# Expert blocks summed in threes, gathers left out of the gates, and part of VectorE's top-k work given to GpSimd

## The chip, the cores and the metric

The kernel runs on one core of one Trainium2 chip, in one launch. The metric is the device time of one execution in microseconds (us). One execution was recorded by the hardware profiler; its rows are the trace. The engines are named as in the profile: PE is TensorE (PEld its weight loads), DVE is VectorE, ACT is ScalarE, POOL is GpSimd, SP is SyncE, which only issues transfers. A q behind the name (POOLq) is the engine's instruction queue. Every engine works through its own queue in order.

## The reference

A decoder layer over x of 1024 tokens by 1024 features. A conditioning vector gives shifts, scales and gates. A first half mixes the tokens (a gated linear recurrence and a short convolution) and adds the result to x. The second half, where the change lies, looks experts up by product keys:

```python
q = (xb @ w_query).reshape(T, PEER_HEADS, 2, PEER_HALF)          # 8 heads, 2 halves of 128
s = jnp.einsum('thpk,hpnk->thpn', q, sub_keys).astype(jnp.float32)  # 128 keys per half
top_s, top_i = lax.top_k(s, PEER_TOPK)                            # 16 of 128
cand_s = top_s[:, :, 0, :, None] + top_s[:, :, 1, None, :]
cand_i = top_i[:, :, 0, :, None] * PEER_NKEYS + top_i[:, :, 1, None, :]
best_s, best_pos = lax.top_k(cand_s.reshape(T, PEER_HEADS, PEER_TOPK * PEER_TOPK), PEER_TOPK)
idx = jnp.take_along_axis(cand_i.reshape(...), best_pos, axis=-1)
gate = jax.nn.softmax(best_s, axis=-1)
u = expert_u[idx]
v = expert_v[idx]
act = jax.nn.gelu(jnp.einsum('td,thkd->thk', xb, u).astype(jnp.float32), approximate=False)
return jnp.einsum('thk,thkd->td', (gate * act).astype(xb.dtype), v)
```

There are 16384 experts (128 by 128), each with a row of 1024 floats in u and one in v; a token uses 128 of them. A last norm follows.

## The kernel before

**Two ways for the tokens.** 640 tokens (TD) go the dense way: u and v of all experts are multiplied for all of these tokens, in 128 blocks of 128 experts, and a matrix of gates that is zero for experts not chosen weighs them. The other 384 tokens go by gathers, in 3 groups of 128: for each of a token's 128 experts an indirect DMA on GpSimd's queue brings the u row (L1095, into one of five row buffers, `grow` and `more`), VectorE multiplies it with the token's h and sums it into `aw` (L1113), and likewise a v row is gathered and added into `gacc` (L1105). That is 384 u steps and 384 v steps of 0.52 MB each. They are written by a generator, `background()`, which other code moves on by `advance(cost)`: with a rate for each stage (RE in the queries, RF in the gates, RG in the tail), and in the main stage by `along`, which spreads what is still left evenly over the matmul columns (`per_column`).

**Products.** A product of two fp32 tiles is three float32r matmuls (high by high, high by low, low by high). `halves_of` makes the halves: ACT copies the raw tile into the high part (L113), DVE subtracts it to get the low part (L114). Names with h and l at the end are such halves: `wh, wl` (or `wxh, wxl` from another pool) of a query weight or of a block of u, `vh, vl` of a block of v, `Wh, Wl` of a block of weighted activations.

**Stages** (names used below, with their place in the trace):
- queries (714 to 857 us): 16 query matrices for the dense tokens, 48 matmuls each on PE (L889), then scores, then the top 16 of 128 on DVE for five tiles of 128 tokens (`top16`, L936 to L940).
- top-k (857 to 989): for each tile the candidates (`candidates`), then softmax, then `digits` for all five tiles in one (it takes the two index digits out of the best positions, in ops of 640 elements), then `pick` for each tile: a one-hot (L1006), a product (L1008), a tree of additions (L1011, L1013). Meanwhile PE computes u blocks that are done early (`u_early`, L1165): 40 of the 128 blocks (EARLIES, every b with b % 3 == 1), stored as `ged` and reloaded in the main stage.
- gates (989 to 1338): ten quarters of 64 tokens. DVE makes one-hots and products (`lo`, `hi`, `O1` at L1303, `P` at L1309), PE multiplies them (L1318, 128 matmuls a quarter), ACT evicts to `stg` and stores to `gd`. Early u blocks and, by RF, gathers are mixed in.
- tail (1338 to 1366): what is left of the early blocks.
- main (1366 to 2989): the u products of the other 88 blocks (L1165), `w_step` (gelu by gate, halves `Wh, Wl`), `v_load` (halves `vh, vl`), and after every SB blocks a `v_phase` that adds Wh, Wl by vh, vl (L1383) for five tiles of tokens: three in PSUM (`pacc`), two through `pa` into `acc0` and `acc2` (L1393). `Wh, Wl, vh, vl` have SLOTS high-part buffers. A phase is written when the next block's W and v have been made.
- end (2989 to 3003).

Order within an engine's queue is set by a scheduler from dependencies and costs; `keep_in_program_order` ties the gathers' steps to the order in which the generator writes them.

Of the kernel before, what the change touches and what calls it, by code (L numbers as in the profile page):

```python
# [7 lines left out]
F32 = mybir.dt.float32  # L8
# [6 lines left out]
OP = mybir.AluOpType  # L15
# [4 lines left out]
P = 128  # L20
S = 1024
DM = 1024
KC = DM // P
# [7 lines left out]
NK = 128  # L31
# [4 lines left out]
DT = -(-TD // P)  # L36
# [2 lines left out]
NG = len(GG)  # L39
FULL = REST // P  # L40
assert REST % P == 0 and TD % P == 0
SB = 4
GB = 4
TG = 64 if TD % 64 == 0 else 32
NTG = TD // TG
GSCALE = 2.0 ** 15
EARLY = 40
EARLIES = [b for b in range(NK) if b % 3 == 1][:EARLY]
SLOTS = SB + 1
ROWS = 4  # L50
TB = 8
NE = 3.6
NF = 2.1
MID = 1
WL = 3
# [22 lines left out]
WH = 3  # L78
WA = 1
RE = 0.1  # L80
RF = 0.9
RG = 0.5
RATES = {"B": RB, "D": RD, "E": RE, "F": RF, "G": RG}
SPREAD = 0.97
# [13 lines left out]
def build(tc, A, out, dbg=None):  # L98
# [9 lines left out]
            return st.enter_context(tc.tile_pool(name=name, bufs=bufs, reuse_waits="tile", **kw))  # L108
        return st.enter_context(tc.tile_pool(name=name, bufs=bufs, side=side, reuse_waits="tile", **kw))

    def split(hi, lo, src):

        C.activation(hi, src, AF.Copy)  # L113
        V.tensor_tensor(lo, src, hi.bitcast(F32), op=OP.subtract)  # L114

    def raw_tile(pl, shape, name, lb):

        return pl.tile(shape, F32R, name=name + "l", bufs=lb).bitcast(F32)

    def halves_of(pl, raw, shape, name, lb, hb):  # L120
        hi = pl.tile(shape, F32R, name=name + "h", bufs=hb)
        lo = pl.tile(shape, F32R, name=name + "l", bufs=lb)
        split(hi, lo, raw)
        return hi, lo

    def rsqrt(r, v, tmp, e=0):
# [13 lines left out]
    with root:  # L140
# [37 lines left out]
        up = pool(stQ, "up", side="right")  # L178
# [17 lines left out]
        def fetch(n):  # L196
            if n < len(order) and n not in raws:
                src, i = order[n]
                raws[n] = raw_tile(up, [P, KC, P], "w", WL)
                SY.dma_start(raws[n], A[src][i])  # L200

        def halve(n):

            if n < len(order) and n not in halves:
                fetch(n)
                if n in extra:
                    halves[n] = halves_of(extra[n], raws[n], [P, KC, P], "wx", 1, 1)
                else:
                    halves[n] = halves_of(up, raws[n], [P, KC, P], "w", WL, 2)

        def deepen(pl, first, n, every):

# [782 lines left out]
            V.tensor_copy(code, ci)  # L995
            return pf, code

        def pick(new, ab, ti, dst):

            w = ti.shape[0]  # L1000
            tib = new("tib", [2, TOPK, HEADS], BF16)
            V.tensor_copy(tib, ti.rearrange("p (h c) a -> p c a h", c=2))
            sh = [w, TOPK, TOPK, HEADS]
            for c in range(2):
                oh = new("oh", [TOPK, TOPK, HEADS], BF16)
                V.tensor_tensor(oh, ab[c][:, :, None, :].to_broadcast(sh),  # L1006
                                iota16[:w, None, :, :].to_broadcast(sh), op=OP.is_equal)
                V.tensor_tensor(oh, oh, tib[:, c, None, :, :].to_broadcast(sh), op=OP.mult)  # L1008
                n = TOPK // 2
                while n > 1:  # L1010
                    V.tensor_tensor(oh[:, :, :n], oh[:, :, :n], oh[:, :, n:2 * n], op=OP.add)  # L1011
                    n //= 2
                V.tensor_tensor(dst[c], oh[:, :, 0], oh[:, :, 1], op=OP.add)  # L1013
                yield 3.5

        def norm_store(pl, o, w, parts, fw, r, sq, queue=None):
# [200 lines left out]
        scores.pop()()  # L1217

        def new(name, shape, dt):
            return qp.tile([P] + shape, dt, name=name, bufs=1)  # L1220

        fill = [0.0, 0.0]

        def early_along(steps_):
            for c in steps_:
                fill[0] += c * NE / 26.0
                if fill[0] - fill[1] > 0.25:
                    u_early(fill[0] - fill[1], "E")
                    fill[1] = fill[0]
# [2 lines left out]
        bp = new("bp", [DT, HEADS, TOPK], U32)  # L1232
        for t in range(DT):
            early_along(candidates(new, lambda v, m, a, b: top16(qp, v, m, a, b), ts[:, t], bs[:, t], bp[:, t]))
        softmax(new, bs, gk)
        ab = digits(new, bp)
        early_along([8.0])
        for t in range(DT):
            early_along(pick(new, [a[:, t] for a in ab], ti[:, t], [i1[:, t], i2[:, t]]))
        stE.close()  # L1240


# [259 lines left out]
```

## Time and profile before

| what | value |
|---|---|
| time, median of 3 runs | 3003.61 us (2998.58 to 3007.3) |
| the profiled execution: time, span in the trace | 3004.52 us, 3002.8 us |
| mean granted TensorE clock | 0.955 |
| busy over the span: PE, DVE, ACT, POOL | 2751.3 us (92%), 2451.9 us (82%), 933.6 us (31%), 1029.8 us (34%) |
| moved by DMA | 767.20 MB, mean 255 GB/s |

The span runs from the first to the last instruction; 1.7 us of the profiled execution lie outside it. A busy share is an average over the stages; the limits differ from stage to stage.

### The profile page before, as it was taken

How to read it: one execution, taken by the hardware profiler on the slowest of the kernel's cores; microseconds unless marked ns; L12 is line 12 of the kernel's file. 1: busy time of each engine (PE TensorE's matmuls, PEld its weight loads, DVE VectorE, ACT ScalarE, POOL GpSimd, SP SyncE). 2: the span in 40 equal slices, each digit the busy share in tenths (PEclk: the TensorE clock that was granted, in tenths of full speed). 3: DMA queues.
4: the chain of work that ended last, by engine and by line, in shares of the span. 5: the costliest groups of instructions: out<-in, count | busy, mean ns of one | idle time of the engine just before them, and what ended most of it. 6: DMA issues, size and time to landing. Idle time of an engine off the chain costs nothing.

```text
span 3002.8 us, 41579 instructions
## 1 busy us (share of the span) xinstructions
PE 2751.3 (92%) x15683; PEld 2432.8 (81%) x15683; DVE 2451.9 (82%) x4997; ACT 933.6 (31%) x1553; POOL 1029.8 (34%) x816
## 2 busy tenths in 40 slices
PE   8999999997999978777999999999999999999998
PEld 5887787877999877676888888888888888888887
DVE  6875529999999989986787878788878788887788
ACT  4643645433222433322222222222121222121222
POOL 0000000000000055553555455555545555555452
PEclk8999999989999988888999999999999999999999
DMA  7424342234234599999898898899888888988885
GB/s 267 148 85 138 132 138 77 71 102 165 64 100 135 198 365 380 374 356 355 314 328 317 296 325 316 316 332 332 321 323 300 311 322 329 334 312 309 311 307 216
DMA packets 249034, 767.20 MB, mean 255 GB/s; under 512 B 23553, under 2 KB 75777, under 8 KB 242434
## 3 DMA queue, kind: packets, MB, share of 16 engines
q0 software_dynamic: 115296, 419.48, 39.0%
q1 hardware_dynamic: 83202, 286.87, 27.2%
q10 hardware_dynamic: 50336, 58.20, 5.5%
q8 instruction: 122, 2.00, 0.3%
q14 instruction: 78, 0.64, 0.1%
HBM read 696.31 MB, written 68.16 MB: 255 GB/s over the span
## 4 chain that ended last, share of the span: by engine, by line
PE 41%; DVE 20%; DMA 15%; issue 15%; POOL 4%; ACT 3%; ACTq 1%; SPq 0%; DVEq 0%; POOLq 0%
PE pacc L1383 10%; PE pa L1383 8%; PE pp L466 7%; PE pa L1165 7%; DMA Wl<-ged 3%; DVE wl L114 3%; DMA wl<-in_uT 2%; DVE gacc L1105 2%; DMA vl<-in_v 2%; PE ps L588 1%; DVE vl L114 1%; PE pp L732 1%; DMA wl<-in_wq 1%; DVE s L938 1%; DVE P L1309 1%
## 5 line engine op out<-in xcount | busy, mean ns | idle before, releaser
L1165 PE MATMUL pa<-h2h,wh 128*128 128x320 f32 x1840 | 582.6, 317 | 44.4 <-ACT ge L1170 32.0
L1165 PE MATMUL pa<-h2h,wl 128*128 128x320 f32 x1840 | 578.3, 315 | 5.1 <-DVE wl L114 5.1
L1165 PE MATMUL pa<-h2l,wh 128*128 128x320 f32 x1840 | 580.3, 315 | 0.0
L1165 PEld LDWEIGHTS pa<-h2h,wh 128*128 128x128 f32 x1840 | 353.7, 192 | 52.4 <-ACT ge L1170 35.2
L1165 PEld LDWEIGHTS pa<-h2h,wl 128*128 128x128 f32 x1840 | 353.2, 192 | 6.3 <-DVE wl L114 6.3
L1165 PEld LDWEIGHTS pa<-h2l,wh 128*128 128x128 f32 x1840 | 354.1, 192 | 2.0
L1383 PE MATMUL pacc<-vh,Wh 128*128 128x512 f32 x768 | 304.7, 397 | 55.0 <-ACT Wh L113 46.4
L113 ACT ACTIVATE wh<-wl 128x1024 fp32r<-128x1024 f32 x187 | 198.0, 1059 | 442.8 <-DMA wl<-in_uT 183.5
L1383 PE MATMUL pacc<-vl,Wh 128*128 128x512 f32 x768 | 301.8, 393 | 0.1
L1383 PE MATMUL pacc<-vh,Wl 128*128 128x512 f32 x768 | 300.3, 391 | 0.1
L114 DVE TENSOR_TENSOR wl<-wl,wh 128x1024 fp32r<-128x1024 f32 x187 | 228.0, 1220 | 75.0 <-ACT wh L113 71.6
L113 ACT ACTIVATE vh<-vl 128x1024 fp32r<-128x1024 f32 x128 | 135.0, 1054 | 370.6 <-PE pacc L1383 297.1
L1383 PE MATMUL pa<-vh,Wh 128*128 128x512 f32 x512 | 206.0, 402 | 24.3 <-ACT Wh L113 22.3
L1383 PEld LDWEIGHTS pacc<-vh,Wh 128*128 128x128 f32 x768 | 145.8, 190 | 92.6 <-ACT Wh L113 55.0
L113 ACT ACTIVATE Wh<-Wl 128x640 fp32r<-128x640 f32 x128 | 94.5, 739 | 380.0 <-DVE Wl L1360 264.7
L1383 PE MATMUL pa<-vl,Wh 128*128 128x512 f32 x512 | 203.9, 398 | 0.0
L1383 PE MATMUL pa<-vh,Wl 128*128 128x512 f32 x512 | 203.3, 397 | 0.0
L1383 PEld LDWEIGHTS pacc<-vh,Wl 128*128 128x128 f32 x768 | 144.9, 189 | 30.8 <-DVE Wl L114 0.8
L1383 PEld LDWEIGHTS pacc<-vl,Wh 128*128 128x128 f32 x768 | 145.8, 190 | 29.5 <-DVE vl L114 0.8
L114 DVE TENSOR_TENSOR vl<-vl,vh 128x1024 fp32r<-128x1024 f32 x128 | 155.0, 1220 | 4.6 <-ACT vh L113 3.7
L466 PE MATMUL pp<-h1h,wh 128*128 128x512 f32 x384 | 157.5, 410 | 0.0
L1318 PE MATMUL pg<-O,P 128*128 128x128 f16 x1280 | 112.9, 238 | 47.2 <-DVE P L1309 44.2
(2071 smaller groups left out, 6599.6 us busy)
## 6 DMA issues: line engine op xcount, KB each, us to landing
wl<-in_uT SPq DMA_DIRECT2D x128, 512.0 KB
vl<-in_v SPq DMA_DIRECT2D x128, 512.0 KB
gd<-stg ACTq DMA_DIRECT2D x10, 4096.0 KB
gsb<-gd SPq DMA_DIRECT2D x32, 1280.0 KB
wl<-in_win SPq DMA_DIRECT2D x48, 512.0 KB
wa<-in_wada SPq DMA_DIRECT2D x16, 1024.0 KB
wl<-in_wq SPq DMA_DIRECT2D x32, 512.0 KB
ged<-ge ACTq DMA_DIRECT2D x40, 320.0 KB
```

What stands on the lines that cost most here:

```text
L113: C.activation(hi, src, AF.Copy)
L114: V.tensor_tensor(lo, src, hi.bitcast(F32), op=OP.subtract)
L466: T.matmul(pp, l[:, k], r[k], start=(i == 0), stop=(i == 3 * KC - 1))
L588: T.matmul(ps_[:, c], X[:, c * P:(c + 1) * P], Xv[:, c, :, 1], start=True, stop=True)
L732: T.matmul(pm, l[:, t * P:(t + 1) * P], r, start=(k == 0 and l is yh[k] and r is woh[k]), stop=(k == KC - 1 and l is yl[k]))
L938: V.match_replace(s2, tsv[:, 0:8], vals, NEG)
L1105: V.scalar_tensor_tensor(ac, r, aw[:, j:j + 1], ac, op0=OP.mult, op1=OP.add))
L1165: T.matmul(pa[:, :n], l[:, k], h2[k, r][:, o:o + n], start=(i == 0), stop=(i == 3 * KC - 1))
L1309: V.tensor_tensor(Pr.rearrange("p g (a b) e -> p g a b e", b=16), gh[r][:, sl, :, None, :].to_broadcast(sh), lo[:, sl, None, :, :].to_broa ...
L1318: T.matmul(pg[:, e_], Ps[r][:, e // 2, :, e % 2], O1[:, e // 2, :, e % 2], start=(r == 0), stop=(r == 1))
L1383: T.matmul(pv, l[:, t * P:(t + 1) * P], r[:, js], start=(i == 0 and (not fx or b0 == 0)), stop=(i == 3 * (b1 - b0) - 1 and (not fx or last)))
```

## The change

Four things change, by constants and by which engine a helper's operations go to.

1. SB goes from 4 to 3, so a `v_phase` sums three blocks; SLOTS is still 5, now SB + 2 instead of SB + 1. Phases other than the last go from 31 to 42, and the additions into `acc0` and `acc2` (four to a phase) from 124 to 168, the first four of them copies. The last phase sums two blocks instead of four.
2. RF goes from 0.9 to 0: no gather steps are written in the gates. `per_column` then spreads them over the main stage.
3. The low parts of the 16 dense query matrices and of the first nine early u blocks are subtracted on GpSimd.
4. `pick` for the dense tokens runs on GpSimd, all but the one-hot; `digits` runs per tile, between the candidates of two tiles, in ops of 128 elements; the temporary tiles get two buffers. The stretches over which early u blocks are handed out in the top-k are shorter (2.0 a tile and 3.0 in place of 8.0 and 3.5 for each of ten picks).

```diff
@@ -39,17 +39,18 @@
 NG = len(GG)
 FULL = REST // P
 assert REST % P == 0 and TD % P == 0
-SB = 4
+SB = 3
 GB = 4
 TG = 64 if TD % 64 == 0 else 32
 NTG = TD // TG
 GSCALE = 2.0 ** 15
 EARLY = 40
 EARLIES = [b for b in range(NK) if b % 3 == 1][:EARLY]
-SLOTS = SB + 1
+SLOTS = SB + 2
 ROWS = 4
 TB = 8
 NE = 3.6
+PE_ = 9
 NF = 2.1
 MID = 1
 WL = 3
@@ -78,7 +79,7 @@
 WH = 3
 WA = 1
 RE = 0.1
-RF = 0.9
+RF = 0.0
 RG = 0.5
 RATES = {"B": RB, "D": RD, "E": RE, "F": RF, "G": RG}
 SPREAD = 0.97
@@ -108,19 +109,19 @@
             return st.enter_context(tc.tile_pool(name=name, bufs=bufs, reuse_waits="tile", **kw))
         return st.enter_context(tc.tile_pool(name=name, bufs=bufs, side=side, reuse_waits="tile", **kw))
 
-    def split(hi, lo, src):
+    def split(hi, lo, src, eng=None):
 
         C.activation(hi, src, AF.Copy)
-        V.tensor_tensor(lo, src, hi.bitcast(F32), op=OP.subtract)
+        (eng or V).tensor_tensor(lo, src, hi.bitcast(F32), op=OP.subtract)
 
     def raw_tile(pl, shape, name, lb):
 
         return pl.tile(shape, F32R, name=name + "l", bufs=lb).bitcast(F32)
 
-    def halves_of(pl, raw, shape, name, lb, hb):
+    def halves_of(pl, raw, shape, name, lb, hb, eng=None):
         hi = pl.tile(shape, F32R, name=name + "h", bufs=hb)
         lo = pl.tile(shape, F32R, name=name + "l", bufs=lb)
-        split(hi, lo, raw)
+        split(hi, lo, raw, eng)
         return hi, lo
 
     def rsqrt(r, v, tmp, e=0):
@@ -203,10 +204,12 @@
 
             if n < len(order) and n not in halves:
                 fetch(n)
+
+                eng = G if 0 <= n - (len(order) - NK - 16) < 16 + PE_ else None
                 if n in extra:
-                    halves[n] = halves_of(extra[n], raws[n], [P, KC, P], "wx", 1, 1)
+                    halves[n] = halves_of(extra[n], raws[n], [P, KC, P], "wx", 1, 1, eng)
                 else:
-                    halves[n] = halves_of(up, raws[n], [P, KC, P], "w", WL, 2)
+                    halves[n] = halves_of(up, raws[n], [P, KC, P], "w", WL, 2, eng)
 
         def deepen(pl, first, n, every):
 
@@ -995,22 +998,22 @@
             V.tensor_copy(code, ci)
             return pf, code
 
-        def pick(new, ab, ti, dst):
+        def pick(new, ab, ti, dst, eng=V):
 
             w = ti.shape[0]
             tib = new("tib", [2, TOPK, HEADS], BF16)
-            V.tensor_copy(tib, ti.rearrange("p (h c) a -> p c a h", c=2))
+            eng.tensor_copy(tib, ti.rearrange("p (h c) a -> p c a h", c=2))
             sh = [w, TOPK, TOPK, HEADS]
             for c in range(2):
                 oh = new("oh", [TOPK, TOPK, HEADS], BF16)
                 V.tensor_tensor(oh, ab[c][:, :, None, :].to_broadcast(sh),
                                 iota16[:w, None, :, :].to_broadcast(sh), op=OP.is_equal)
-                V.tensor_tensor(oh, oh, tib[:, c, None, :, :].to_broadcast(sh), op=OP.mult)
+                eng.tensor_tensor(oh, oh, tib[:, c, None, :, :].to_broadcast(sh), op=OP.mult)
                 n = TOPK // 2
                 while n > 1:
-                    V.tensor_tensor(oh[:, :, :n], oh[:, :, :n], oh[:, :, n:2 * n], op=OP.add)
+                    eng.tensor_tensor(oh[:, :, :n], oh[:, :, :n], oh[:, :, n:2 * n], op=OP.add)
                     n //= 2
-                V.tensor_tensor(dst[c], oh[:, :, 0], oh[:, :, 1], op=OP.add)
+                eng.tensor_tensor(dst[c], oh[:, :, 0], oh[:, :, 1], op=OP.add)
                 yield 3.5
 
         def norm_store(pl, o, w, parts, fw, r, sq, queue=None):
@@ -1217,7 +1220,7 @@
         scores.pop()()
 
         def new(name, shape, dt):
-            return qp.tile([P] + shape, dt, name=name, bufs=1)
+            return qp.tile([P] + shape, dt, name=name, bufs=1 if name in ("cand", "bs", "bp", "be", "sm") else 2)
 
         fill = [0.0, 0.0]
 
@@ -1232,11 +1235,12 @@
         bp = new("bp", [DT, HEADS, TOPK], U32)
         for t in range(DT):
             early_along(candidates(new, lambda v, m, a, b: top16(qp, v, m, a, b), ts[:, t], bs[:, t], bp[:, t]))
+            ab = digits(new, bp[:, t:t + 1])
+            early_along([2.0])
+            for _ in pick(new, [a[:, 0] for a in ab], ti[:, t], [i1[:, t], i2[:, t]], G):
+                pass
         softmax(new, bs, gk)
-        ab = digits(new, bp)
-        early_along([8.0])
-        for t in range(DT):
-            early_along(pick(new, [a[:, t] for a in ab], ti[:, t], [i1[:, t], i2[:, t]]))
+        early_along([3.0])
         stE.close()
```

Lines of the kernel after stand one further down than before from L114 on, three from the halving of the next weights on, four from the gates on. Where the orders show a place, names as `grow__10157` are single buffers of a kind.

The first place is POOL's queue in the queries stage, from the first u gathers on. Before:

```order
L1095 DMA grow__10157<-in_u,idx 128x1024
L1095 DMA grow__10201<-in_u,idx 128x1024
L1095 DMA grow__10211<-in_u,idx 128x1024
L1095 DMA more<-in_u,idx 128x1024
L1095 DMA grow__10232<-in_u,idx 128x1024
L1087 DMA hx<-h2d 128x1024
L1095 DMA grow__10280<-in_u,idx 128x1024
L1247 IOTA di 128x256
L1095 DMA grow__10330<-in_u,idx 128x1024
```

After, from the third query's low part on (`wl<-wl,wh` is the subtraction of L114):

```order
L115 TENSOR_TENSOR wl<-wl,wh 128x1024 x6
L1098 DMA grow__13626<-in_u,idx 128x1024
L1098 DMA grow__13640<-in_u,idx 128x1024
L115 TENSOR_TENSOR wl<-wl,wh 128x1024 x2
L1098 DMA grow__13652<-in_u,idx 128x1024
L1098 DMA more<-in_u,idx 128x1024
L115 TENSOR_TENSOR wl<-wl,wh 128x1024
L1090 DMA hx<-h2d 128x1024
L1098 DMA grow__13655<-in_u,idx 128x1024
L115 TENSOR_TENSOR wl<-wl,wh 128x1024
L1098 DMA grow__13681<-in_u,idx 128x1024
L115 TENSOR_TENSOR wl<-wl,wh 128x1024 x6
```

The first gathers of group 1, which wait for their indices and buffers, now stand between the low parts that the queries' matmuls need.

The second place is DVE's queue in the middle of the gates. Before:

```order
L1303 TENSOR_TENSOR O_12122<-iT,ramp 128x1024
L1309 TENSOR_TENSOR P_12124<-gh,lo 128x1024
L1309 TENSOR_TENSOR P_12126<-hi,lo 128x1024
L1105 SCALAR_TENSOR_TENSOR gacc<-grow__12148,aw,gacc 128x1024
L1113 SCALAR_TENSOR_TENSOR grow__12160,aw<-grow__12160,hx 128x1024
L1303 TENSOR_TENSOR O_12169<-iT,ramp 128x1024
L1309 TENSOR_TENSOR P_12171<-gh,lo 128x1024
L1309 TENSOR_TENSOR P_12173<-hi,lo 128x1024
L1105 SCALAR_TENSOR_TENSOR gacc<-grow__12195,aw,gacc 128x1024
L1113 SCALAR_TENSOR_TENSOR more,aw<-more,hx 128x1024
```

After:

```order
L1307 TENSOR_TENSOR O_8617<-iT,ramp 128x1024
L1313 TENSOR_TENSOR P_8621<-hi,lo 128x1024
L1307 TENSOR_TENSOR O_8658<-iT,ramp 128x1024
L1313 TENSOR_TENSOR P_8660<-gh,lo 128x1024
L1313 TENSOR_TENSOR P_8662<-hi,lo 128x1024
L1307 TENSOR_TENSOR O_8709<-iT,ramp 128x1024
L1313 TENSOR_TENSOR P_8711<-gh,lo 128x1024
L1313 TENSOR_TENSOR P_8713<-hi,lo 128x1024
L1307 TENSOR_TENSOR O_8752<-iT,ramp 128x1024
L1313 TENSOR_TENSOR P_8754<-gh,lo 128x1024
```

The two gather steps that stood after nearly every set of `O` and `P` are gone.

The third place is ACT's queue in the main stage, over about three blocks. Before:

```order
L113 ACTIVATE Wh<-Wl 128x640
L1170 ACTIVATE Wl<-pa 128x320 x2
L113 ACTIVATE Wh<-Wl 128x640
L113 ACTIVATE vh<-vl 128x1024
L1170 ACTIVATE Wl<-pa 128x320
L113 ACTIVATE vh<-vl 128x1024
L113 ACTIVATE wh<-wl 128x1024
L1170 ACTIVATE Wl<-pa 128x320
L113 ACTIVATE vh<-vl 128x1024
L113 ACTIVATE Wh<-Wl 128x640
L113 ACTIVATE wh<-wl 128x1024
L113 ACTIVATE Wh<-Wl 128x640
```

After (L1173 is the gelu of L1170):

```order
L114 ACTIVATE Wh<-Wl 128x640
L1173 ACTIVATE Wl<-pa 128x320 x2
L114 ACTIVATE vh<-vl 128x1024
L114 ACTIVATE wh<-wl 128x1024
L114 ACTIVATE Wh<-Wl 128x640
L1173 ACTIVATE Wl<-pa 128x320 x2
L114 ACTIVATE vh<-vl 128x1024
L114 ACTIVATE wh<-wl 128x1024
L114 ACTIVATE Wh<-Wl 128x640
L114 ACTIVATE vh<-vl 128x1024
L1124 ACTIVATE aw<-aw 128x32
L114 ACTIVATE Wh<-Wl 128x640
```

Before, two or three `vh` stand close together and a `vh` may stand ahead of two `Wh`; after, a block's gelus, `vh`, `wh` and `Wh` follow each other in a nearly regular row.

## Rows read from the trace of the kernel before

**Rows 1.** Cores: span, mean granted TensorE clock

```profile
core 0: 3002.8 us, clock 0.955
```

**Rows 2.** Windows by stage: us; PE, PEld, DVE, ACT, POOL busy; PEclk, DMA share, GB/s

```profile
714.00:857.00 143.00, 137.91 (x946) 135.48 (x945) 139.33 (x750) 33.56 (x60) 4.76 (x3) 0.97 0.30 100
857.00:989.00 132.00, 121.93 (x785) 119.86 (x784) 128.06 (x538) 35.50 (x58) 3.27 (x4) 0.95 0.37 118
989.00:1047.00 58.00, 54.70 (x579) 49.37 (x578) 55.37 (x101) 32.39 (x62) 1.48 (x1) 0.97 0.64 214
1047.00:1338.00 291.00, 224.63 (x1771) 203.84 (x1770) 273.58 (x417) 93.51 (x172) 159.85 (x123) 0.84 1.00 369
1338.00:1366.00 28.00, 14.36 (x94) 14.10 (x95) 17.19 (x21) 3.64 (x7) 16.37 (x13) 0.83 1.02 387
1366.00:2989.00 1623.00, 1530.65 (x8064) 1357.10 (x8062) 1310.77 (x1640) 386.05 (x556) 829.13 (x641) 0.98 0.88 316
```

**Rows 3.** Windows, DVE busy at L1113 alone (gathered u), two instructions a step

```profile
989.00:1340.00 351.00, 94.76 (x156) 0.86 0.94 343
1366.00:2989.00 1623.00, 366.80 (x600) 0.98 0.88 316
```

**Rows 4.** Windows, DVE busy at L1105 alone (gathered v)

```profile
989.00:1340.00 351.00, 58.08 (x46) 0.86 0.94 343
1366.00:2989.00 1623.00, 423.36 (x330) 0.98 0.88 316
```

**Rows 5.** Windows, PE and PEld busy at L1318 alone (gates)

```profile
989.00:1047.00 58.00, 31.66 (x399) 23.92 (x398) 0.97 0.64 214
1047.00:1338.00 291.00, 81.02 (x880) 60.84 (x880) 0.84 1.00 369
```

**Rows 6.** PE's waits, 980 to 1395 us: total, times, longest

```profile
PE pg L1318 <- DVE P L1309: 44.2, 40, 6.3
PE pa L1165 <- ACT ge L1170: 29.4, 11, 13.2
```

**Rows 7.** PE's waits in the main stage, 1395 to 2950 us

```profile
PE pacc L1383 <- ACT Wh L113: 46.4, 20, 4.8
PE pa L1383 <- ACT Wh L113: 21.6, 9, 5.7
```

**Rows 8.** ACT's waits in the main stage, 1395 to 2950 us

```profile
ACT vh L113 <- PE pacc L1383: 297.1, 20, 21.9
```

**Rows 9.** DVE's groups in the top-k, 857 to 981 us: busy, mean ns

```profile
L1008 DVE TENSOR_TENSOR oh<-oh,tib 128x2048 bf16<-128x2048 bf16 x10 | 12.2, 1224 | 0.3
...
L984 DVE TENSOR_SCALAR ctmp<-pf 128x640 bf16<-128x640 bf16 x7 | 3.5, 507 | 0.1
...
L1013 DVE TENSOR_TENSOR i<-oh 128x128 f32<-128x128 bf16 x10 | 2.9, 292 | 0.3
...
L1002 DVE CAST tib<-ti 128x256 bf16<-128x256 uint32 x5 | 1.9, 388 | 0.0
```

**Rows 10.** Window, DVE busy at L1011 alone (additions of pick)

```profile
857.00:981.00 124.00, 15.44 (x33) 0.97 0.38 121
```

**Rows 11.** Windows, DVE busy at L114 alone (low parts)

```profile
714.00:857.00 143.00, 21.18 (x23) 0.97 0.30 100
866.00:989.00 123.00, 19.51 (x16) 0.94 0.38 122
```

**Rows 12.** Timeline of POOL: start us, us, instruction

```profile
917.10 0.79 POOL L1247 IOTA di<- 128x256 int32 x1
```

**Rows 13.** Instructions of L275: duration ns min/median/max, first and last start

```profile
L275 POOL IOTA jp<- x1: 225/225/225, 0.8 to 0.8; 128x128 int32 x1
```

**Rows 14.** POOL's groups: busy, mean ns, idle before and releaser

```profile
L1095 POOL DMA_INDIRECT more<-in_u,idx x76 | 103.5, 1362 | 100.9 <-DVE gacc L1105 56.5 <-DVE more L1113 25.5 <-issue 10.0
...
L1095 POOL DMA_INDIRECT grow__10211<-in_u,idx x1 | 1.9, 1871 | 121.0 <-DVE ts L939 121.0
```

**Rows 15.** Timeline of PE: first matmul of the eleventh query

```profile
807.64 0.31 PE L889 MATMUL pq<-h2h,wh 128*128 128x320 f32 x1
```

**Rows 16.** Timeline of DVE: last index of the ninth query's top 16

```profile
808.27 0.28 DVE L940 FIND_INDEX8 ti<-ts,s 128x8 uint32<-128x128 f32 x1
```

**Rows 17.** Window, DVE busy at L1393 alone (additions into acc0, acc2)

```profile
1366.00:2989.00 1623.00, 82.07 (x120) 0.98 0.88 316
```

## The prediction

> **What bounds the kernel now.** I read the cores row first: one core at a mean granted clock of 0.955 [rows 1], so the clock is not the story of the whole, though it is of one stage. Then the windows by stage [rows 2], since each stage has another limit. In the queries PE (138 of 143 us) and DVE (139) are both full. In the top-k DVE is (128 of 132), and PE is kept busy by early u blocks. The gates fall into two parts: up to 1047 us, while no gathers come, PE and DVE are both at 95% and the clock is 0.97; from 1047 on gathers come, DVE is at 94% (274 of 291), DMA is full (share 1.00) at 369 GB/s, PE is busy 77% of the time, the granted clock falls to 0.84 of the upper level, 2.4 GHz, and a matmul of the gates takes 92 ns (81.02/880) where it took 79 (31.66/399) [rows 5]. PE's waits there are for DVE's `P` (44.2 us) and for gelus (29.4 us, one of 13.2) [rows 6]. In the main stage PE is busy 1531 of 1623 us, DVE 1311, DMA 0.88; PE's largest waits are for ACT's `Wh` at the start of a phase: 46.4 and 21.6 us, 29 times, that is nearly once a phase [rows 7].
>
> **The change part by part.** The sum is made against the profiled execution, 3004.5 us, 0.9 above the median of the runs.
>
> *Queries.* The low parts leave DVE (21 us [rows 11]) and become 16 operations on POOL, which is busy only 5 of 143 us. PE is as full as DVE, so DVE's relief buys at most a few us. But the order puts gathers between them: those ahead of the eleventh, twelfth and thirteenth low part wait for the last steps of the gathers' own top-k on DVE, which stand behind the ninth and tenth query's top 16. Now one such gather waited 121 us with only gathers behind it [rows 14]; after, low parts that PE needs stand there. The ninth query's top 16 ends at 808.5 us [rows 16], the eleventh query starts at 807.6 [rows 15]. Behind that end come some DVE steps of pick, two gathers of 1.4 us [rows 14] and a subtraction, 8 to 10 us, once; the next two are late by the same stretch, not by another. I take +10, between 0 (slack) and +20 (twice).
>
> *Top-k.* DVE loses the product, the additions, the last addition and the cast of pick: 12.2 + 14.0 (30 of the 33 at L1011) + 2.9 + 1.9 = 31 us [rows 9, 10], and most of its low parts (14 of 16, 17 us [rows 11]). Digits in 24 small operations a tile cost more than 24 large ones together: 507 ns is one of 640 elements, 292 the last addition of 128 [rows 9]; taking 0.2 us for a digit's operation of 128, below that row since its types are narrower, 120 make 24 us against some 13 for the 24 large ones; +11. DVE is left with 128 - 31 - 17 + 11 = 91 us. POOL now has the long chain: per tile 2 x (2048 + 1024 + 512 + 256 + 128) + 256, some 8200 elements a partition. The trace has no such operation on POOL. The nearest rows are its two iotas: 0.225 us for 128 elements, 1.8 ns each [rows 13], and 0.79 us for 256, 3.1 ns each [rows 12]; the other end is DVE's own price, 31/5 = 6.2 us a tile. I take 2.4 ns, the middle of the iotas: 19.7 us a tile, plus 2.5 for a low part between two tiles, 108 us in all. The chain starts when the first tile's digits and one-hot are done: queries' end 867, 9 us of top 16 left, 11 of candidates, 5 of digits, 1 of one-hot, so 893; it ends at 1001, and ramp, transposes and the first `O` and `P` take some 8 more (now the same way from 981 to 989). The gates would begin near 1009 instead of 989: +20, of which 10 are the queries'. Bounds: at DVE's price DVE sets the end, 867 + 91, or -23 for the top-k; at 3.1 ns +40. PE stands idle for part of it, because fewer early blocks are written here (510 matmuls by the orders before the first gate product, 768 now).
>
> The Trainium skill (GPSIMD Engine Reference, section 3.1, on elementwise work side by side) gives 4497 ns for an addition of 2048 fp32 elements on GpSimd against 2293 on VectorE; no run here shows it yet. By that, an estimate, a tile would take 18 us and the gates begin 8 us sooner than I say.
>
> *Gates.* Their 78 u and 46 v steps go: 94.8 + 58.1 = 153 us of DVE [rows 3, 4] and the transfers with them. DVE keeps 55.4 + 273.6 - 152.8 = 176 us [rows 2]. PE needs 1280 gate products of 79 ns and some 915 early matmuls (by the order) of 150 ns (137.9/946 = 146 in the queries, 121.9/785 = 155 in the top-k [rows 2]): 101 + 137 = 238 us. So PE sets it, as it nearly does in the 58 us without gathers: that stretch ran three quarters at 19 us each with 59 early matmuls a quarter; 92 a quarter give 24. I take 240 where there are 349: -109, between 215 (fewer early matmuls fit) and 265 (PE waits for `P` and for gelus as before).
>
> *Tail.* The early blocks that were not done in the top-k come here: 399 matmuls by the order against 94 [rows 2], 60 us against 28, of which 14 were waits for a stored gelu: +32, between +25 and +50.
>
> *Main stage.* Its matmuls are the same: 1531 us. A phase of three needs three `Wh` and `vh`, and the five buffers now leave room for two blocks ahead, not one. ACT's `vh` copies wait 297 us for PE to release buffers [rows 8], and `Wh` stands behind them in the same queue; with the second spare buffer and the regular order most of PE's 68 us for `Wh` [rows 7] should go. That is the gain. Against it, DVE takes the gates' gathers: 83 u steps of 1.22 us (366.8/300) and 54 v steps of 1.28 (423.4/330) [rows 3, 4], and 44 additions of 0.68 us (82.07/120 [rows 17]): 101 + 69 + 30 = 200, so 1511 us. At the 94% that DVE reached in the gates this is 1607 us. DMA moved 316 GB/s x 1623 us = 513 MB; 137 gathers of 0.52 MB make 585, 1585 us at 369 GB/s. PE alone: 1531 and the 24 us of idle time that the two groups of waits don't explain, 1555. Three engines within 3% of each other get in each other's way, so I take a value just above the largest, 1615: -8. Bounds: 1555 and 1740, the latter with DVE at 87%, between its 81% now and the 94%.
>
> Sum: 3004.5 + 10 + 10 - 109 + 32 - 8 = 2939.5; against the median, 2939. So most of the gates' gain is meant to survive because the main stage has room on DVE (19%) and DMA (12%) that the gates did not have.
>
> **Rivals.** *The main stage is PE's alone* (1555): the waits go and DVE follows. For it: DVE's idle time there is 312 us, the added work 200. Then 2880. *The main stage can't take the gathers.* DVE works in order, and each gather step waits for its row; if it does not get above 90% busy, 1511/0.9 = 1680, the gain is gone: the point of no change is 1615 + 65 = 1680. For it: 81% now, 1.00 of DMA to be reached, where a gather's row comes late. Against it: the gates ran at 94% with DMA full. At 87% it would be 1740, and the time 3064: this is the rival on the other side. *GpSimd's operations and DVE's can't run together.* If each of DVE's two-input operations in the top-k has to wait for a running one on POOL, the two add up: 91 + 108 us from 876 instead of overlapping, so the gates begin at 1083 at the worst, +74, half of it if half overlaps: 2976 to 3013. No row shows the two together.
>
> The Trainium skill (SBUF - State Buffer, section on the two separate sides) says that a VectorE operation with two SBUF inputs and a GpSimd operation that reads SBUF share one port pair as an exclusive lock, held for the whole instruction. By it this rival would come true as far as the one-hots, the small additions and the subtractions go; the top 16 has one input and would run on.
>
> That the change doesn't do what it says is excluded for the gates: the order shows not one gather step in them.
>
> **How the numbers follow.** Main stage and top-k about as forecast, 2900 to 2965: 0.52. PE alone, 2850 to 2900: 0.17. Gathers not taken, from 2965 up: 0.19. Lock, 2965 to 3015: 0.12. The range 2868 to 2998 leaves out a third of the second (0.06) and most of the third above (0.13). For this kernel 0.3%, 9 us, is about what a measurement can tell from no change. Below 2994.6 lie the first two, 0.07 of the lock and 0.03 of the third: 0.79; within 9 us of 3003.6 lies 0.08; above, 0.13.
>
> **What would show it.** Queries: a POOL subtraction idle behind a gather's wait, and PE waiting for `wl` in the eleventh query. Top-k: POOL's product of 2048 at 4 to 6 us, and DVE's one-hots waiting for POOL's release of `oh`. Gates: quarters of 24 us, clock above 0.95, no DMA at 1.00. Main: PE's waits for `Wh` well under 68 us, DVE at 92 to 95%, 360 GB/s or more. I am wrong if the main stage is over 1680 us or the gates start after 1050.

## The result, and the profile after

The kernel after took 3107.76 us in the median of 4 runs (3106.51 to 3118.02) against 3004.7 for the kernel before: 1.0358 times as long, with a 95% interval of 1.0332 to 1.0384. I had forecast 2939 us, a gain, so the sign was wrong, and 103 us are to be explained. The profiled execution has a span of 3105.6 us at a mean granted clock of 0.952, hardly another clock than before [rows 1].

The windows of the kernel after, cut at its own stages (queries, top-k, gates, tail, main stage, end), answer to the stages of before [rows 2]. The columns are those of that group.

```profile
714.00:859.00 145.00, 137.89 (x949) 134.97 (x948) 136.76 (x738) 34.04 (x61) 43.85 (x22) 0.98 0.33 113
859.00:1021.00 162.00, 90.02 (x527) 88.22 (x525) 148.10 (x554) 26.81 (x42) 112.40 (x64) 0.76 0.17 57
1021.00:1260.00 239.00, 233.02 (x2307) 220.78 (x2306) 188.53 (x316) 123.10 (x229) 0.00 (x0) 1.00 0.71 236
1260.00:1339.00 79.00, 73.94 (x493) 73.42 (x491) 13.03 (x12) 18.72 (x31) 0.00 (x0) 0.98 0.58 200
1339.00:3084.00 1745.00, 1563.90 (x7968) 1362.50 (x7968) 1479.46 (x1868) 376.46 (x546) 1045.77 (x776) 0.96 0.90 329
3084.00:3105.00 21.00, 0.00 (x0) 0.00 (x0) 17.32 (x62) 4.15 (x12) 0.00 (x0) 0.60 0.31 125
```

To set tail and main stage beside these, the kernel before has to be cut at the same events (last gate product, first matmul of a phase), not at 1366 us as above. These are two windows of the trace of before:

```profile
1338.00:1390.00 52.00, 30.23 (x188) 29.70 (x188) 28.23 (x34) 7.50 (x13) 23.15 (x19) 0.81 1.01 388
1390.00:2989.00 1599.00, 1514.78 (x7968) 1341.49 (x7968) 1299.74 (x1627) 382.19 (x550) 822.36 (x635) 0.98 0.88 314
```

By stage, from the window lengths: queries +2 (143 to 145), top-k +30 (132 to 162), gates -110 (349 to 239), tail +27 (52 to 79), main stage +146 (1599 to 1745), end +7 (14 to 21); together +102. The gates gave what was forecast, to 1 us. The main stage took all of it back and 36 us more, and top-k, tail and end add the rest. (With the main stage begun where the prediction begins it, at the first of its own u blocks, the tail is +38, from 28 to 66, and the main stage +135, from 1623 to 1758.)

In the main stage both PE and DVE have idle time: PE is busy 1564 of 1745 us, DVE 1479. PE's largest waits (trace of after, 1355 to 3050 us: total, times, longest) are now spread over several releasers, where before 68 of some 83 us were for `Wh` [rows 7]:

```profile
PE pacc L1387 <- ACT Wh L114: 67.5, 25, 10.2
PE pa L1387 <- DVE acc L1397: 34.0, 20, 5.2
PE pa L1387 <- ACT Wl L1173: 24.0, 14, 4.0
PE pa L1168 <- ACT Wl L1173: 18.6, 10, 5.3
PE pa L1168 <- DVE acc L1397: 15.0, 16, 2.2
PE pa L1168 <- DVE wl L115: 14.9, 13, 3.6
```

The waits for `acc` are new: PE stands because DVE has not yet added a finished `pa`, so DVE's queue is late. The waits for `Wh` have not gone, 67.5 us at `pacc` alone, but their reason has changed, as ACT's waits in the same window show:

```profile
ACT Wh L114 <- DVE Wl L1364: 794.0, 98, 22.8
...
ACT vh L114 <- PE pacc L1387: 35.1, 5, 12.8
```

ACT's wait for a buffer of `vh`, 297 us before [rows 8], is down to 35, as the second spare buffer should do. In its place ACT waits for DVE's `Wl`, and PE's `Wh` with it.

What makes DVE late is seen in the timelines of the kernel after, DVE first, then POOL (start, length, instruction, and idle time before it with its releaser):

```profile
1627.16 1.28 DVE L1108 SCALAR_TENSOR_TENSOR gacc<-grow__15406,aw,gacc 128x1024 f32<-128x1024 f32 x1
1628.36 1.22 DVE L1116 SCALAR_TENSOR_TENSOR grow__15425<-grow__15425,hx 128x1024 f32<-128x1024 f32 x1
1629.50 0.08 DVE L1116 DVE_READ_ACCUMULATOR grow__15425<-grow__15425,hx 128x1 f32 x1
1630.54 1.28 DVE L1108 SCALAR_TENSOR_TENSOR gacc<-grow__15441,aw,gacc 128x1024 f32<-128x1024 f32 x1 [0.95 <-DMA grow__15441<-in_v,idx]
1632.22 1.22 DVE L1116 SCALAR_TENSOR_TENSOR more<-more,hx 128x1024 f32<-128x1024 f32 x1 [0.40 <-DMA more<-in_u,idx]
```

```profile
1617.77 1.69 POOL L1098 DMA_INDIRECT grow__15425<-in_u,idx  x1 [1.78 <-DVE gacc L1108]
1619.77 0.95 POOL L1098 DMA_INDIRECT grow__15441<-in_v,idx  x1 [0.30 <-issue]
1621.02 1.57 POOL L1098 DMA_INDIRECT more<-in_u,idx  x1 [0.31 <-issue]
1622.90 0.95 POOL L1098 DMA_INDIRECT grow__15482<-in_v,idx  x1 [0.30 <-DVE vl L115]
1628.71 1.69 POOL L1098 DMA_INDIRECT grow__15494<-in_u,idx  x1 [4.86 <-DVE gacc L1108]
```

POOL needs 1.3 to 2.0 us for a gather (in these rows 0.95 to 1.7 us of issue, and 0.3 us before the next), DVE 1.2 to 1.3 us to use one. The row for which DVE waits 0.95 us at 1630.54 was issued at 1619.77, 10.8 us before, and the one at 1632.22 was issued 11.2 us before. The median row takes 6.6 us from the start of its issue to its landing, and a slow one is late, however early POOL was. Nor could POOL run further ahead: with five rows out it has no buffer left, and it idles (4.86 us before 1628.71) until DVE has used a row. So a row buffer goes round a loop: issue on POOL, transfer, its turn in DVE's queue, use, release; 762 rows in 1745 us are one in 2.29 us, or 11.5 us a round of the five. Summed over all instructions at the two lines in the main stage, DVE's idle time before them is 133 us in the kernel before and 185 us after; DVE's idle time before everything else falls from 168 to 81.

The chain that ended last shows the same change of hands. These are its shares of the span by engine, before and after; the one of after goes back only to 1210 us, which is why it adds up to 61%:

```profile
PE 41%; DVE 20%; DMA 15%; issue 15%; POOL 4%; ACT 3%; ACTq 1%; SPq 0%; DVEq 0%; POOLq 0%
```

```profile
DMA 21%; issue 12%; DVE 11%; POOL 9%; PE 7%; ACT 1%; ACTq 0%; SPq 0%; DVEq 0%; POOLq 0%
```

Within the main stage alone PE's share falls from 47% to 7%, and DMA, DVE and POOL together rise from 38% to 71%.

### The profile page after: what moved, and what is told of

Read it like the earlier page. It is cut to its first block, busy times and chain, and to the rows that moved or that the text cites. A ratio compares the mean times of both kernels' runs of the same rounds, so it can differ in the third digit from the quotient of the medians.

```text
span 3105.6 us, 41786 instructions
## 1 busy us (share of the span) xinstructions
PE 2769.7 (89%) x15683; PEld 2437.4 (78%) x15683; DVE 2504.2 (81%) x5057; ACT 929.8 (30%) x1553; POOL 1220.5 (39%) x896
## 4 chain that ended last, share of the span: by engine, by line
DMA 21%; issue 12%; DVE 11%; POOL 9%; PE 7%; ACT 1%; ACTq 0%; SPq 0%; DVEq 0%; POOLq 0%
PE pa L1168 4%; DMA more<-in_v,idx 4%; DVE gacc L1108 3%; DMA wl<-in_uT 3%; POOL more L1098 2%; DMA more<-in_u,idx 1%; DVE vl L115 1%; DVE Wl L1364 1%; PE pa L1387 1%; PE pacc L1387 1%; DVE wl L115 1%; DVE Wl L115 1%; DMA vl<-in_v 1%; DMA grow__21361<-in_u,idx 0%; DVE acc L1397 0%
## 5 line engine op out<-in xcount | busy, mean ns | idle before, releaser
L1168 PE MATMUL pa<-h2h,wh 128*128 128x320 f32 x1840 | 590.8, 321 | 38.9 <-ACT Wl L1173 18.6
L1387 PE MATMUL pacc<-vh,Wh 128*128 128x512 f32 x768 | 305.3, 402 | 70.3 <-ACT Wh L114 67.5
L114 ACT ACTIVATE wh<-wl 128x1024 fp32r<-128x1024 f32 x187 | 197.8, 1058 | 485.5 <-DMA wl<-in_uT 276.7
L114 ACT ACTIVATE Wh<-Wl 128x640 fp32r<-128x640 f32 x128 | 94.1, 736 | 804.3 <-DVE Wl L1364 804.3
L115 DVE TENSOR_TENSOR wl<-wl,wh 128x1024 fp32r<-128x1024 f32 x165 | 207.2, 1256 | 98.6 <-ACT wh L114 98.0
L1387 PEld LDWEIGHTS pa<-vh,Wh 128*128 128x128 f32 x512 | 99.0, 193 | 96.3 <-DVE acc L1397 45.8
L115 DVE TENSOR_TENSOR vl<-vl,vh 128x1024 fp32r<-128x1024 f32 x128 | 155.8, 1217 | 20.3 <-ACT vh L114 20.1
L114 ACT ACTIVATE vh<-vl 128x1024 fp32r<-128x1024 f32 x128 | 135.1, 1056 | 119.3 <-DMA vl<-in_v 84.0
```

The costliest lines, as they stand in the source:

```text
L115: (eng or V).tensor_tensor(lo, src, hi.bitcast(F32), op=OP.subtract)
L1168: T.matmul(pa[:, :n], l[:, k], h2[k, r][:, o:o + n], start=(i == 0), stop=(i == 3 * KC - 1))
L1387: T.matmul(pv, l[:, t * P:(t + 1) * P], r[:, js], start=(i == 0 and (not fx or b0 == 0)), stop=(i == 3 * (b1 - b0) - 1 and (not fx or last)))
```

## The experiments

Three questions: which part of the change costs how much; what limits the main stage once all gathers are in it; what made the top-k longer. Twelve kernels ran. Ratios are against runs of the kernel before on the same chip, with 95% intervals; the medians of before in the different sets of runs lie between 3001.7 and 3006.7 us, so a difference of two kernels' times is uncertain by some 5 us beyond their own spread. "Main stage" is always from the first matmul of a phase to the last matmul.

**Only the gates without gathers (b_rf0)**, from the kernel before:

```diff
-RF = 0.9
+RF = 0.0
```

> The kernel before with RF = 0 alone: no gathers in the gates, phases of four, VectorE's top-k as before. If the moved gathers are what lengthens the main stage (theory G), the gates fall by about 110 us and the main stage grows from 1623 to about 1745, total about 3015 us. If phases of three are what lengthens it (rival S), the main stage has room for the gathers and grows by 30 to 40 us only, total about 2930 us.

3047.58 us, 1.0150 (1.0107 to 1.0194). Gates 231 us, main stage 1763:

```profile
987.00:1218.00 231.00, 225.52 (x2253) 213.26 (x2252) 185.86 (x315) 121.03 (x226) 0.00 (x0) 1.00 0.71 239
1265.00:3028.00 1763.00, 1577.10 (x7967) 1378.83 (x7966) 1460.79 (x1835) 381.10 (x549) 1022.08 (x776) 0.95 0.89 326
```

Theory G holds, and the price is above its forecast: the main stage grows by 164 us, the gates give 118.

**Only phases of three (b_sb3)**, from the kernel before:

```diff
-SB = 4
+SB = 3
-SLOTS = SB + 1
+SLOTS = SB + 2
```

> The kernel before with SB = 3 and SLOTS = SB + 2 alone, gathers in the gates as before. Theory G: the main stage stays at 1623 us or gains up to 60 from the shorter waits for Wh, total 2945 to 3005 us. Rival S: the 44 more additions and the phases' shorter runs of matmuls lengthen the main stage to about 1720, total about 3100 us.

2980.45 us, 0.9922 (0.9895 to 0.9949): a gain of 26 us, main stage 1576. Rival S falls. PE's waits in it show that those for `Wh` are gone, and that waits for gelus have come in their place:

```profile
PE pa L1383 <- ACT Wl L1170: 53.7, 33, 3.9
PE pa L1165 <- ACT Wl L1170: 5.9, 4, 4.2
```

**After, with gathers in the gates (a_rf9)**:

```diff
-RF = 0.0
+RF = 0.9
```

> The kernel after with RF = 0.9 again, all else as after. Theory G: the gates go back to about 350 us from 239 and the main stage to about 1625 from 1758, total about 3085 us, so what is left of the loss (about 80 us) is the top-k and the early blocks moved out of it. Rival S: the gates grow by 110 us and the main stage hardly falls, total about 3190 us.

3050.77 us, 1.0151 (1.0116 to 1.0187): 57 us below the kernel after. Main stage 1561, gates 364. It fell further than theory G said, because the main stage falls by 184 us and not by 133.

**After, with phases of four (a_sb4)**:

```diff
-SB = 3
+SB = 4
-SLOTS = SB + 2
+SLOTS = SB + 1
```

> The kernel after with SB = 4 and SLOTS = SB + 1 again, all else as after. Theory G: the main stage stays within 30 us of 1758, total 3080 to 3140 us. Rival S: it falls to about 1650, total about 3000 us.

3136.13 us, 1.0432 (1.0379 to 1.0484): 28 us above the kernel after, main stage 1782. So phases of three gain about as much here as from the kernel before, though this run is the most scattered (3118 to 3145 us) and 26 us of its main stage are PE's own: 1590 us busy against 1564, at a granted clock of 0.93 against 0.96. What the other parts of the change cost follows: from b_sb3 to a_rf9, which differ by parts 3 and 4 of the change (low parts, top-k and early blocks), 70 us; gathers out of the gates 57; phases of three -26 to -28; together some 100 of the 103 us, as steps that lead from one kernel to the other must. So the largest price is that of the work given to GpSimd and the early blocks moved, of which 52 us were forecast (queries, top-k and tail); the gathers moved had been forecast as a large gain.

**Half of VectorE's work on gathered rows (a_half)**, from the kernel after:

```diff
-V.scalar_tensor_tensor(ac, r, aw[:, j:j + 1], ac, op0=OP.mult, op1=OP.add))
+V.scalar_tensor_tensor(ac[:, :512], r[:, :512], aw[:, j:j + 1], ac[:, :512], op0=OP.mult, op1=OP.add))
-V.scalar_tensor_tensor(r, r, 1.0, hx, op0=OP.mult, op1=OP.mult,
+V.scalar_tensor_tensor(r[:, :512], r[:, :512], 1.0, hx[:, :512], op0=OP.mult, op1=OP.mult,
```

> The kernel after, with VectorE working on 512 of the 1024 columns of each gathered row (u sums and v additions leave out the other half); every gather still brings the whole row. It tells apart what the main stage waits for. If VectorE's time is the limit there (theory D: 768 steps of 1.25 us fall to about 0.65), the main stage falls from 1745 us, first phase to last matmul, to PE's own 1560 to 1600, total about 2940 us. If the rate at which rows can be fetched into five buffers is the limit (rival R: 46 to 48 gathers in 100 us), it stays above 1680, total 3050 us or more.

3022.70 us, 1.0070 (1.0045 to 1.0094). The window of its main stage:

```profile
1337.00:3010.00 1673.00, 1539.72 (x7967) 1350.44 (x7966) 1090.34 (x1878) 379.36 (x549) 878.01 (x776) 0.97 0.92 343
```

DVE lost 389 us of work (1479 to 1090), the stage only 72 (1745 to 1673, between the two forecasts and nearer to the rival's 1680; the total, too, lies between them). DVE is now idle 404 us before gathered rows alone. So most of what limits the stage is the coming of the rows, not DVE's time on them. Even the 72 us are not DVE's time alone: POOL's busy time fell as well, from 1046 to 878 us, and the median issue of a gather from 1.43 to 0.97 us (last section).

**One more row buffer (a_rows5)**, from the kernel after:

```diff
-ROWS = 4
+ROWS = 5
```

> The kernel after with one more row buffer for the gathers (ROWS = 5, six in all). Theory D: VectorE's waits for gathered rows, 185 us of the main stage, fall by a third at most, 1745 to about 1690, total 3050 to 3105 us. Rival R: the rate of gathers rises with the buffers, the main stage falls to about 1600, total about 2960 us.

3010.39 us, 1.0029 (1.0010 to 1.0048): 97 us less than the kernel after, from 4 KB a partition.

```profile
1342.00:2998.00 1656.00, 1541.45 (x7968) 1348.69 (x7968) 1471.94 (x1869) 377.49 (x547) 1035.68 (x775) 0.98 0.93 346
```

DVE does the same work (1472 us); its idle time before gathered rows falls from 185 to 83 us, and the stage by 89. The total lies inside neither forecast but well below theory D's, and the waits fall by more than half where D allowed a third; so DVE's time is not the whole limit. The stage's 1656 us is still nearer to D's 1690 than to R's 1600: R holds in its direction, not in its size.

**Both (a_half_rows5)**: the diffs of a_half and a_rows5.

> The kernel after with six row buffers and VectorE working on 512 of 1024 columns of each gathered row (the other half of the u sums and v additions is left out). Theory R: with rows fetched faster and VectorE free, the main stage falls to 1570 to 1600 us from 1656 with six buffers and 1674 with half the work, total about 2940 us. Rival (DMA full at 352 GB/s and a share of 0.95 sets the end): it stays at 1640 or more, total about 3000 us.

2952.15 us, 0.9831 (0.9806 to 0.9856), main stage 1593, as R forecast, at 360 GB/s and a DMA share of 0.95, so 1656 is not DMA's floor. With six buffers, taking DVE's work away brings 63 us more, nearly the 72 that it brought with five. The gains almost add (89 and 72 alone, 152 together), as terms of one loop would; which of them comes first the runs don't tell.

**Pick on VectorE again (a_pickv)**, from the kernel after:

```diff
-            for _ in pick(new, [a[:, 0] for a in ab], ti[:, t], [i1[:, t], i2[:, t]], G):
+            for _ in pick(new, [a[:, 0] for a in ab], ti[:, t], [i1[:, t], i2[:, t]]):
```

> The kernel after with pick on VectorE again, digits still per tile and the low parts still on GpSimd. If GpSimd's chain of picks sets the end of the top-k (theory P), the stage falls from 162 us to 125 to 135, and since the tail keeps its 399 early matmuls the total falls by 30 us, to about 3075 us. Rival: the small digit operations on VectorE and the waits for low parts set it, and the stage stays at 150 to 165 us, total 3100 us.

3065.95 us, 1.0217 (1.0174 to 1.0259): 42 us less than the kernel after. The top-k falls from 162 to 122 us, 10 less than in the kernel before:

```profile
862.00:984.00 122.00, 89.95 (x587) 87.15 (x586) 120.20 (x607) 28.07 (x45) 20.40 (x9) 0.87 0.27 82
```

So GpSimd's chain of picks, with what it holds up on VectorE, does set the length of the top-k in the kernel after; the tail stays at 80 us.

**More early blocks in the top-k (a_fill3)**, from the kernel after:

```diff
-            early_along([2.0])
+            early_along([8.0])
-        early_along([3.0])
+        early_along([12.0])
```

> The kernel after with more early u blocks handed out in the top-k (8.0 a tile and 12.0 at the end in place of 2.0 and 3.0; by the order 648 early matmuls stand ahead of the first gate product, 510 in the kernel after, 768 before). If PE's idle time in the top-k (72 of 159 us) is simply room that early blocks can fill, the top-k keeps its length and tail or gates fall by 138 x 0.15 = 21 us, total about 3085 us. Rival: the early blocks wait for low parts that stand behind the picks on GpSimd, the top-k grows by as much, total 3105 us.

3120.22 us, 1.0389 (1.0345 to 1.0432). The tail falls from 79 to 35 us, but the gates grow to 270, the top-k to 173 and the main stage to 1757. Of the 268 matmuls that left the tail 135 show in the top-k and 128 in the gates. PE's busy time in the top-k rose by 28 us and the stage by 11, so its idle time is room in part; but of the tail's 44 us nothing is left, since the top-k (11), the gates (31) and the main stage (12) grew by more. The rival had the direction; its reason, the low parts behind the picks, was not tested by itself.

**One more row buffer in the kernel before (b_rows5)**:

```diff
-ROWS = 4
+ROWS = 5
```

> The kernel before with one more row buffer alone (ROWS = 5, six in all). If late rows cost the main stage time only when all gathers are in it (theory R1), little changes here, 2990 to 3004 us. If the five buffers already limited the main stage of before (R2; VectorE waited 133 us for rows there), it falls by 30 us or more, total below 2980 us.

2953.69 us, 0.9842 (0.9814 to 0.9870); main stage 1564 from 1599. R2 holds: late rows cost time before the change already, and DVE's idle time before them falls from 133 to 62 us.

**Phases of three and one more buffer (b_sb3_rows5)**: the diffs of b_sb3 and b_rows5.

> The kernel before with phases of three (SB = 3, SLOTS = SB + 2) and one more row buffer; gathers in the gates and VectorE's top-k as before. If the two gains add, from 2980 us with phases of three alone by what the buffer alone gives; total 2940 to 2975 us, the fastest so far. Rival: the main stage is then PE's alone and the buffer gives nothing more, 2975 to 2985 us.

2916.19 us, 0.9724 (0.9702 to 0.9747). This lies below both forecasts. The two gains add (26 and 48 alone, 85 together, the 11 us above their sum being within the intervals), and this is the fastest kernel of the study. PE is busy 98% of its main stage:

```profile
1375.00:2895.00 1520.00, 1493.05 (x7967) 1329.18 (x7968) 1311.49 (x1649) 383.17 (x547) 834.25 (x634) 0.99 0.90 329
```

**The same without gathers in the gates (b_sb3_rf0_rows5)**: as b_sb3_rows5, and RF = 0.0.

> The kernel before with phases of three, no gathers in the gates and one more row buffer; the top-k on VectorE as before. Against the kernel after with that buffer (3010 us) it leaves out only the work given to GpSimd and the early blocks moved, so theory P (these cost some 60 to 70 us in top-k and tail) gives about 2945 us; it also tells whether moving the gathers out of the gates pays with six buffers: yes if it is below the kernel with phases of three, six buffers and gathers in the gates. If P is wrong, about 3000 us.

2942.96 us, 0.9813 (0.9790 to 0.9836). Against a_rows5 it is 67 us faster: theory P holds. Against b_sb3_rows5 it is 27 us slower: the gates give 113 us (344 to 231), the main stage takes 131 (1520 to 1651). Moving the gathers does not pay with six buffers either.

## Why the prediction was wrong

- **Gates, right, to 1 us by luck.** 240 us forecast, 239 measured, with no gather and PE busy 97% at a granted clock of 1.00, the upper level of 2.4 GHz (0.84 before, while gathers came). DVE's work was 189 us where I had 176. Two errors met: 1018 early matmuls fell in the stage where I had 915, but they took 138 ns each (233 less the gate products' 93 us) where I had 150, and a gate product 72 ns where I had 79.
- **Tail, right in size.** +32 forecast; +27 by the cut used here, +38 by the prediction's own.
- **Queries, over-sized.** +10 forecast, +2 measured: PE is busy 137.9 of 145 us there, as before, so the low parts behind the gathers came in time.
- **Top-k, too small.** The gates were to start at 1009 us and started at 1021. POOL's prices were well sized: the two products of a tile take 9.1 us, the six additions 7.7, the last two 0.8, the cast 0.6, a low part 2.3, together 20.5, where I had 22. But the products start at 886, 913, 939, 966 and 994 us, 26 to 28 apart: I let DVE's digits run beside POOL's chain, and most of them stand still while it works (last section). So POOL idles 6.2 us in three of the tiles and 7.8 in the last, 26 us in all, until DVE has finished the next digits and one-hot. (The lower of the bounds there was also uneven: the -23 at DVE's price holds the queries' +10, the +40 does not.)
- **Main stage, the step that failed:** "At the 94% that DVE reached in the gates this is 1607 us", and from it the 1615. DVE was busy 85% (1479 of 1745). The work was sized rightly: 200 us more than before were forecast, 188 came (1309 to 1497 in main stage and end). But I took from the gates the share that DVE reached, and not the rate of the rows. The gates took 124 rows in 291 us, one in 2.35 us, with DMA full; 1615 us for the 762 rows of the main stage ask for one in 2.12 us, faster than the gates or the main stage of the kernel before (2.57) had shown, where the quickest 60 in a row took 2.27 each; and the stage reached 2.29. (The rate in the gates was not set by the buffers: with six they take 344 us in b_sb3_rows5, with five 345 in b_sb3.) What holds the rate in the main stage is the loop of five row buffers: release by DVE, issue on POOL, transfer, use. I had POOL's waits for a release in a row (100.9 us before the u rows in `more` alone [rows 14]) and used that row for the issue time only. The runs show that the loop is the cause: one buffer more takes 89 us off the stage with DVE's work unchanged (one row in 2.17 us), half of DVE's work on the rows only 72, both together 152. By the prediction's own cut the stage was forecast at -8 us and came out at +135: 143 of the 168 us between forecast and result.
- **The gain of the phases, right in kind, less than half in size:** from the kernel before, the waits for `Wh` go (68 us there, none listed in b_sb3), and phases of three alone gain 26 us, not 68, since waits for gelus (60 us) come next. In the kernel after the gain is still there (28 us against a_sb4), but the sign I had named, waits for `Wh` well under 68 us, is not: they are 67.5 us, now behind DVE's late `Wl`.
- **The rivals.** The one on the other side, that the main stage can't take the gathers, is what happened: 87% and 1740 us were its figures, 85% and 1745 came by the cut from the first phase. I gave it 0.19 because of the 94% in the gates. Its total of 3064 lacked, in the main, the top-k's extra 20 us, the end's 7 and, by the prediction's cut, 18 of the main stage. The rival of GpSimd and VectorE excluding each other is seen too, as 26 us of POOL's idle time, below its 37 to 74, and nothing in it was run by itself. By the lock that the Trainium skill describes (SBUF - State Buffer, the section on the two separate sides) DVE operations with two SBUF inputs or in a two-port mode would wait. The trace agrees on the sums, which have two, and the top 16, with one input, ran on as the prediction said; whether the cast, the copies and the digit operations, which were held too, ran in a two-port mode no row shows. The Trainium skill's 4497 ns for an addition of 2048 fp32 elements (GPSIMD Engine Reference, section 3.1) stands beside some 4.6 us for a product of 2048 bf16 elements here (9.1 for two), and the prediction's estimate from it, 18 us a tile, beside 18.2 (9.1, 7.7, 0.8 and 0.6).

Open: in the kernel after, DVE's first gather step of the main stage comes at 1390.0 us, 51 us after the first phase began, while POOL has waited 377.3 us for it; how much of the 146 us this late start is was not tried. It is there, 48 to 74 us after the first phase, in every kernel without gathers in the gates, also in a_half_rows5 (52 us), whose main stage is 1593 us; in those with gathers in the gates the steps run through. It is the same with six buffers (51 us in a_rows5), so it is no part of what the sixth gained. A seventh buffer was not tried either; SBUF has no room for it here.

## What to carry to other kernels

Moving work from a stage where an engine is full to one where it is 81% busy is worth nothing if the idle share there is made of waits that the moved work itself brings. Ask what paces that work (here a loop of five buffers through GpSimd, the DMA and VectorE) and count its rate, before counting the engine's time; compare the rate that the new stage asks for (here a row in 2.12 us) with the fastest that a stage of the trace shows (2.35). One more buffer in the loop was worth more than any other single change tried that keeps the result: 48 us in the kernel before, 97 in the kernel after. And work handed to GpSimd was not off VectorE's path as long as VectorE had sums and copies to do in the same stretch: the picks alone, handed back, gained 42 us.

## What the runs showed of the hardware

Most of VectorE's operations in the top-k stand still while GpSimd computes in SBUF, and not only those with two inputs. In the kernel after, in the second and third tile of the top-k (timeline of POOL, then of DVE, same columns as above; the DVE operations between those shown are left out):

```profile
912.96 9.10 POOL L1011 TENSOR_TENSOR oh<-oh,tib 128x2048 bf16<-128x2048 bf16 x2 [6.18 <-DVE oh L1009]
922.01 7.65 POOL L1014 TENSOR_TENSOR oh<-oh 128x1024 bf16<-128x1024 bf16 x6
929.62 0.81 POOL L1016 TENSOR_TENSOR i<-oh 128x128 f32<-128x128 bf16 x2
930.39 2.34 POOL L115 TENSOR_TENSOR wl<-wl,wh 128x1024 fp32r<-128x1024 f32 x1
932.67 0.62 POOL L1005 CAST tib<-ti 128x256 bf16<-128x256 uint32 x1
939.48 9.05 POOL L1011 TENSOR_TENSOR oh<-oh,tib 128x2048 bf16<-128x2048 bf16 x2 [6.19 <-DVE oh L1009]
```

```profile
918.22 3.92 DVE L958 TENSOR_TENSOR cand<-ts 128x64 f32<-128x64 f32 x1
922.06 2.19 DVE L982 CAST pf<-bp 128x128 bf16<-128x128 uint32 x1
...
926.20 1.17 DVE L985 COPY code<-pf 128x128 bf16<-128x128 bf16 x1
...
930.42 2.36 DVE L987 TENSOR_SCALAR ctmp<-pf 128x128 bf16<-128x128 bf16 x1
...
933.56 0.18 DVE L987 TENSOR_SCALAR ctmp<-pf 128x128 bf16<-128x128 bf16 x1
933.77 0.22 DVE L988 TENSOR_TENSOR code<-code,ctmp 128x128 bf16<-128x128 bf16 x1
...
938.17 1.23 DVE L1009 TENSOR_TENSOR oh<-pf,iota 128x2048 bf16<-128x2048 bf16 x1
```

The sum `cand<-ts` ends with POOL's second product (922.1 and 922.0 us), the cast with its first addition, the one at 930.42 with its subtraction (932.8 and 932.7). From 933.3 us on POOL has nothing to do, and the same digit operations take 0.18 to 0.22 us. With pick on VectorE (a_pickv) the cast takes 0.264 us in the median and the copy 0.195. The searches of the top 16 (MAX8, FIND_INDEX8) keep their 0.20 us beside POOL's work.

The other way round, VectorE lengthens GpSimd's issue of a gather. In the main stage of the kernel after, an issue that begins while VectorE is idle takes 0.95 us in the median (117 of them, none above 0.98), and as long beside VectorE's additions `acc<-acc,pa`, one of whose inputs lies in PSUM (64). Beside operations with both inputs in SBUF it is longer: 1.50 and 1.58 us beside the two kinds of gather step (177 and 193), 1.57 beside the subtractions at L115 (128). So VectorE's work on the rows also slows the fetching of the next ones. What this is worth in the stage no run shows by itself.
